# Score and broadcast products on 128 rows instead of 64 or 4, with the local-attention scores as hi/lo sums

## The chip, the cores and the metric

The kernel runs on one core of one Trainium2 chip. It computes two layers of one model and one layer of a second for 256 tokens in a single launch. The metric is the device time of one execution in microseconds, as the median of several runs.

## The reference, cut to what matters

The inputs are 256 tokens of 1024 channels, float32 throughout. Each layer is a chain of large products (feed-forward blocks of 2816 hidden channels, projections in and out) around a token mixer. Three mixers matter here.

Layer A is an mLSTM: its scores are weighted by `exp` of a running maximum of gate sums, for 4 heads, and that maximum (a row of 256 tokens for each head) has to reach all 128 rows of keys.

Layer B is a sliding-window attention with 16 query heads of 64 channels, in two groups of 8 that share one key head each. A block of 128 queries sees its own block of keys and the one before it:

```python
s = jnp.einsum('bqhgd,bkhd->bhgqk', qn, kn)
s = jnp.where(valid, s, -jnp.inf)
m = jnp.maximum(jnp.max(s, axis=-1, keepdims=True), sink)
p = jnp.exp(s - m)
denom = jnp.sum(p, axis=-1, keepdims=True) + jnp.exp(sink - m)
return jnp.einsum('bhgqk,bkhd->bqhgd', p / denom, vn)
```

The second model's layer is a state-space mixer (SSD) with 32 heads of 64 channels, whose scores are weighted by a decay between two tokens:

```python
acum = jnp.cumsum(dtc * a, axis=1)
seg = acum[:, :, None] - acum[:, None, :]
decay = jnp.exp(jnp.where(causal, seg, -jnp.inf))
...
scores = cb[..., None] * decay
```

## The kernel before

Weights come from memory in chunks of 128 x 1024 elements through SyncE's queue (`load`, L314), five chunks ahead. `prepare` splits each chunk into `hi`, a rounded copy in the type fp32r, by ScalarE (L324), and `lo`, the rest, by VectorE (recorded at the helper's line L122). Activations are split in the same way. A large product is then three fp32r matmuls into one PSUM bank: hi by hi, hi by lo, lo by hi. `gemm` does so with tokens as the stationary side and 512 moving columns (L418 to L420), `gemm_ch` with channels as the stationary side and 256 moving columns (L440 to L442). A product of plain float32 operands, without the split, appears in the trace as two matmul passes; an fp32r product and a transpose (L453, L625, against `ident`) appear as one.

Everything else is called side work. `later` queues generators, `defer` delays a function by a number of ticks, and `gemm` and `gemm_ch` call `tick` between their chunks, which runs what is due and takes steps of the generators at a set `pace`. `pipeline` starts one unit at each step and moves a started unit on every second step. The framework then orders each engine's instructions with this program order as their priority, so that a transpose can land in the middle of another unit's score products. Each engine executes its own list in order.

Three kinds of side product use fewer than 128 rows of TensorE's array, that is, operands that lie on fewer than 128 partitions:

- L1010 in `swa_units`, the scores of layer B. A unit takes heads of one parity, because two heads share a 128-row transposed block: even heads lie on rows 0 to 63 and odd heads on rows 64 to 127. `kv_evac` puts the keys on both halves (`kd`, L966), transposes them and copies them into `bkt` (L971), `bq_evac` transposes the queries and copies them (L983). Both are plain float32. The first block of queries (t = 0) sees 128 keys and has two units of four heads for each group, the second (t = 1) sees 256 and has four units of two heads. With two groups that makes four units of the first kind and eight of the second.
- L806 in `score_head`: the row of running maxima of head `hh`, one of the first 4 rows of `m_t`, is spread over 128 rows by a one-hot stationary operand.
- L1227 in `ssd_unit`: the cumulated decays `act_t` (hi parts on 32 rows, lo parts on the next 32) are spread in the same way by a column of `pick`, twice in each of 16 units. `step_chain` makes `act_t` by a product with the identity (L1124) and a copy.

After the scores, a unit of layer B takes the masked maximum (L1013, VectorE), the exponential (L1019, ScalarE), four transposes (L625) and the products with the values (L1032). All of this draws on one pool of 31 slots of 128 x 512 elements (`slot`); powers for the norms run on GpSimd (L504, L508).

Of the kernel before, what the change touches and what calls it, by code (L numbers as in the profile page):

```python
# [17 lines left out]
P = 128  # L18
# [44 lines left out]
class Operand:  # L63
    """A transposed activation, rows of K on the partitions, as an exact sum hi + lo."""
# [11 lines left out]
class Chunk:  # L76
    """One weight transfer of 1024 elements a partition and the products its columns take part in."""
# [8 lines left out]
def hybrid_kernel(ctx: ExitStack, tc: tile.TileContext, *aps, names=None):  # L86
# [54 lines left out]
    # ------------------------------------------------------------ constants  # L141
# [23 lines left out]
    # parameters by channel, transposed once  # L165
# [33 lines left out]
    # rows on every partition  # L199
# [3 lines left out]
    # ------------------------------------------------------------ weights  # L203
# [131 lines left out]
    # Work that the products hide: steps of generators and delayed calls, taken between the chunks.  # L335
# [38 lines left out]
    def pipeline(units, dist):  # L374
        """Starts a unit at each step; a unit goes on to its next stage every dist steps."""
# [15 lines left out]
    def gemm(chunks, xop, evac, groups=None, by_key=False):  # L391
        """Token-major products: evac(tok, key, psum) after each accumulation."""
# [36 lines left out]
    def gemm_ch(chunks, xop, evac):  # L429
        """Channel-major products of 512 columns: evac(pair, psum) with two tiles of 128 channels."""  # L430
# [17 lines left out]
    # ------------------------------------------------------------ activations  # L448
    def split_t(src, nk, dsts):
        """src [tokens, nk*128] transposed, as hi and lo in dsts (APs of [P, nk, 128])."""  # L450
        ps = bank()
        for i in range(nk):
            pe.transpose(out=ps[:, i * P:(i + 1) * P], in_=src[:, i * P:(i + 1) * P], identity=ident)  # L453
        v = ps[:, 0:nk * P].rearrange("p (a b) -> p a b", a=nk)
        act.copy(out=dsts[0], in_=v)
        tt(dsts[1], v, dsts[0].bitcast(F32), ALU.subtract)
# [9 lines left out]
    def direct_block(op, tok, k0, ps, nk):  # L466
        """An operand from a psum that already holds it transposed."""
# [7 lines left out]
    class NormT:  # L475
        """The normed residual, transposed, for products of either kind."""
# [23 lines left out]
    def inv_rms(sums):  # L500
        """(sums[0] + sums[1] + EPS) ** -0.5 of two columns"""
# [8 lines left out]
    def normed(src, gains, put):  # L510
        """src(j) are the two halves of a row; put(j, normed half)"""
# [20 lines left out]
    def residual_gemm(chunks, xop, scale, after, tail=TAIL):  # L532
        """residual += scale * product; after(tok) when a tile is whole"""
# [15 lines left out]
    def norm_after(row, queue=nc.sync):  # L549
        """An operand to be filled by the gemm before, and the function that fills it."""  # L550
# [25 lines left out]
    def log1p_small(o, e, n):  # L576
        """log(1 + e) for 0 <= e <= 1, as 2 atanh(e / (2 + e))"""
# [18 lines left out]
    # ------------------------------------------------------------ memory attention  # L596
# [3 lines left out]
    def head_norm(pieces, n_heads, d):  # L600
        """rms over each head of d columns, of psum pieces side by side; returns a slot"""
# [58 lines left out]
    def mem_unit(t, hp, queries, po, y, k0):  # L660
        """two heads of the attention over the memory for one tile of tokens"""
# [37 lines left out]
    # ------------------------------------------------------------ first block  # L699
# [29 lines left out]
    # ---- layer A: mLSTM  # L729
# [17 lines left out]
    m_t = slot()  # L747

# [51 lines left out]
    def score_head(hh):  # L800
# [5 lines left out]
        pe.matmul(out=bc[:, 0:SEQ], lhsT=ident[0:4, hh:hh + 1].to_broadcast([4, P]), rhs=m_t[0:4, 0:SEQ],  # L806
# [79 lines left out]
    # ---- rotary tables  # L886
# [44 lines left out]
    # ---- layer B: sliding window attention  # L931
    def rope(x3, t, nh):
        """x3 [P, nh, 64] in place"""
# [22 lines left out]
    bkt, bv = slot(), slot()  # L956
# [3 lines left out]
    def kv_evac(t, key, ps):  # L960
# [8 lines left out]
        def go():  # L969
            tk = transposes(kd, 2)  # L970
            dve.tensor_copy(out=bkt.rearrange("p (g t) -> p g t", g=2)[:, :, t * P:(t + 1) * P],  # L971
                            in_=tk[:, 0:SEQ].rearrange("p (g t) -> p g t", g=2))
# [3 lines left out]
    def bq_evac(g):  # L976
        def evac(t, key, ps):
            qn = qk_norm(ps, t, 8, b_gq)

            def go():  # L980
                tq = transposes(qn, 4)
                q = slot()
                act.copy(out=q, in_=tq)  # L983
                qts[t, g] = q
# [3 lines left out]
    def swa_units(t, g):  # L988
        """eight heads of one key head for one block of queries, a bank of scores at a time"""
# [4 lines left out]
        sets = [[h0 + par + 2 * i for i in range(per)] for h0 in range(0, 8, 2 * per) for par in range(2)]  # L994
# [3 lines left out]
        def unit(n, hs):  # L998
            while (t, g) not in qts or len(kv_ready) <= t:
                yield  # L1000
            qt = qts[t, g]
# [5 lines left out]
            cols = slice(hs[0], hs[-1] + 1, 2)  # L1007
            for i, hh in enumerate(hs):
                half = slice(64 * (hh % 2), 64 * (hh % 2) + 64)
                pe.matmul(out=s[:, i * w:(i + 1) * w], lhsT=qt[half, (hh // 2) * P:(hh // 2 + 1) * P],  # L1010
                          rhs=bkt[half, g * SEQ:g * SEQ + w], start=True, stop=True)
# [47 lines left out]
    # ------------------------------------------------------------ second block  # L1059
# [12 lines left out]
    acs = const.tile([P, 2, 2, 32], F32R, name="acs")  # L1072
    act_t = const.tile([64, SEQ], F32R, name="act_t")
    pick = const.tile([64, 32], F32R, name="pick")
# [18 lines left out]
    def step_chain():  # L1093
# [29 lines left out]
        for c in range(2):  # L1123
            pe.matmul(out=at_[0:64, c * P:(c + 1) * P], lhsT=acs[:, c, :, :].rearrange("p b c -> p (b c)"), rhs=identr,  # L1124
                      start=True, stop=True)
        act.copy(out=act_t, in_=at_[0:64, 0:SEQ])
        tt(pick, ident[0:64, 0:32], ident[0:64, 32:64], ALU.add)
# [5 lines left out]
    def conv_silu(ps, tile_i, dst):  # L1133
        """four taps along the tokens, bias and silu: dst [P, SEQ]"""
# [82 lines left out]
    def ssd_unit(g, hp):  # L1217
        """the decays of two heads over both blocks of tokens, and what they give within a block"""
# [178 lines left out]
```

## Time and profile before

| what | value |
|---|---|
| median of 3 runs | 1620.25 us (1619.86 to 1621.65) |
| span of the profiled execution | 1618.5 us (the page lists its span alone, no other time of it) |
| TensorE matmul busy | 1599.2 us, 99% |
| TensorE weight load busy | 1339.0 us, 83% |
| VectorE busy | 966.7 us, 60% |
| ScalarE busy | 822.5 us, 51% |
| GpSimd busy | 40.7 us, 3% |
| TensorE's part of the chain that ended last | 94% |
| mean granted TensorE clock | 0.997 of full speed |

Matmuls are pipelined, so the duration of one overlaps the next. What one costs in a stream is read from the distance between the starts of neighbours, not from its duration. In the timeline view neighbours of one line are merged into one row, with their count behind the x and the time from the first start to the last end as its length. The forms such as 64\*128 give the rows and columns of the array that the instruction uses.

### The profile page before, as it was taken

How to read it: one execution, taken by the hardware profiler on the slowest of the kernel's cores; microseconds unless marked ns; L12 is line 12 of the kernel's file. 1: busy time of each engine (PE TensorE's matmuls, PEld its weight loads, DVE VectorE, ACT ScalarE, POOL GpSimd, SP SyncE). 2: the span in 40 equal slices, each digit the busy share in tenths (PEclk: the TensorE clock that was granted, in tenths of full speed). 3: DMA queues.
4: the chain of work that ended last, by engine and by line, in shares of the span. 5: the costliest groups of instructions: out<-in, count | busy, mean ns of one | idle time of the engine just before them, and what ended most of it. 6: DMA issues, size and time to landing. Idle time of an engine off the chain costs nothing.

```text
span 1618.5 us, 21426 instructions
## 1 busy us (share of the span) xinstructions
PE 1599.2 (99%) x8124; PEld 1339.0 (83%) x8124; DVE 966.7 (60%) x1372; ACT 822.5 (51%) x1170; POOL 40.7 (3%) x72
## 2 busy tenths in 40 slices
PE   9999999999999999999999999999999999999998
PEld 7888898788888888888788888889899988888886
DVE  6555475558555555546765655368788864575552
ACT  6444365546444444444564544357856553454442
POOL 0000010100000000001100000000000000000000
PEclk9999999999999999999999999999999999999999
DMA  8665374446656566564333766565455566466560
GB/s 271 209 188 196 115 263 144 156 130 211 192 184 196 168 197 187 188 196 164 122 88 108 223 193 195 156 197 184 156 158 145 155 195 182 156 221 188 188 198 27
DMA packets 126971, 282.80 MB, mean 175 GB/s; under 512 B 12286, under 2 KB 23698, under 8 KB 126868
## 3 DMA queue, kind: packets, MB, share of 16 engines
q1 hardware_dynamic: 126868, 281.43, 55.0%
q8 instruction: 64, 1.05, 0.3%
q14 instruction: 39, 0.32, 0.1%
HBM read 280.34 MB, written 1.05 MB: 174 GB/s over the span
## 4 chain that ended last, share of the span: by engine, by line
PE 94%; DVE 2%; issue 1%; ACT 1%; DMA 1%; POOL 1%; SPq 0%; POOLq 0%; ACTq 0%; DVEq 0%
PE ps L418 25%; PE ps L420 25%; PE ps L419 25%; PE ps L440 3%; PE ps L441 3%; PE ps L442 3%; PE ps L453 3%; DMA raw<-in_ffn_w_in_dram 1%; PE ps L625 1%; PE ps L1010 1%; PE ps L1252 1%; POOL t L508 1%; PE ps L1032 1%; DVE wlo L122 1%; ACT whi L324 1%
## 5 line engine op out<-in xcount | busy, mean ns | idle before, releaser
L122 DVE TENSOR_TENSOR wlo<-raw,whi 128x1024 fp32r<-128x1024 f32 (+1 forms) x521 | 628.5, 1213 | 440.3 <-ACT whi L324 433.8
L324 ACT CAST whi<-raw 128x1024 fp32r<-128x1024 f32 (+1 forms) x521 | 543.0, 1044 | 556.4 <-PE ps L420 474.3
L418 PE MATMUL ps<-whi,xh 128*128 128x512 f32 (+2 forms) x1168 | 459.5, 394 | 3.0 <-DVE s L122 1.5
L420 PE MATMUL ps<-whi,xl 128*128 128x512 f32 (+2 forms) x1168 | 451.3, 387 | 0.3 <-DVE xl L122 0.2
L419 PE MATMUL ps<-wlo,xh 128*128 128x512 f32 (+2 forms) x1168 | 450.8, 386 | 0.0
L418 PE MATMUL ps<-whi,s 128*128 128x512 f32 x696 | 278.9, 401 | 0.3 <-ACT s L1329 0.3
L419 PE MATMUL ps<-wlo,s 128*128 128x512 f32 x696 | 274.5, 394 | 0.0
L420 PE MATMUL ps<-whi,s 128*128 128x512 f32 x696 | 274.1, 394 | 0.0
L418 PEld LDWEIGHTS ps<-whi,xh 128*128 128x128 f32 x1168 | 219.7, 188 | 48.1 <-DVE s L122 2.3
L420 PEld LDWEIGHTS ps<-whi,xl 128*128 128x128 f32 x1168 | 219.5, 188 | 45.9 <-DVE xl L122 0.9
L419 PEld LDWEIGHTS ps<-wlo,xh 128*128 128x128 f32 x1168 | 219.9, 188 | 41.5 <-issue 0.3
L420 PEld LDWEIGHTS ps<-whi,s 128*128 128x128 f32 x696 | 130.7, 188 | 30.7
L418 PEld LDWEIGHTS ps<-whi,s 128*128 128x128 f32 x696 | 130.8, 188 | 30.4 <-ACT s L1329 0.8
L419 PEld LDWEIGHTS ps<-wlo,s 128*128 128x128 f32 x696 | 130.9, 188 | 28.7
L440 PE MATMUL ps<-xh,whi 128*128 128x256 f32 x448 | 129.8, 290 | 0.0
L441 PE MATMUL ps<-xl,whi 128*128 128x256 f32 x448 | 127.6, 285 | 0.0
L442 PE MATMUL ps<-xh,wlo 128*128 128x256 f32 x448 | 127.6, 285 | 0.0
L440 PEld LDWEIGHTS ps<-xh,whi 128*128 128x128 f32 x448 | 86.4, 193 | 1.7 <-issue 0.2
L441 PEld LDWEIGHTS ps<-xl,whi 128*128 128x128 f32 x448 | 86.4, 193 | 0.4 <-issue 0.2
L442 PEld LDWEIGHTS ps<-xh,wlo 128*128 128x128 f32 x448 | 86.2, 193 | 0.1
L453 PE MATMUL ps<-ident,s 128*128 128x128 f32 x444 | 66.7, 274 | 2.0 <-DVE s L131 2.0
L453 PEld LDWEIGHTS ps<-ident,s 128*128 128x128 f32 x444 | 54.3, 141 | 16.4 <-issue 1.9
(211 smaller groups left out, 971.8 us busy)
## 6 DMA issues: line engine op xcount, KB each, us to landing
raw<-in_ffn_w_in_dram SPq DMA_DIRECT2D x160, 512.0 KB, 4.7
raw<-in_ffn_w_out_dram SPq DMA_DIRECT2D x88, 512.0 KB, 3.4
raw<-in_w_in_dram SPq DMA_DIRECT2D x80, 512.0 KB, 4.1
raw<-in_a_w_in_dram SPq DMA_DIRECT2D x24, 512.0 KB, 4.6
raw<-in_w_gate_dram SPq DMA_DIRECT2D x44, 256.0 KB, 3.1
raw<-in_w_up_dram SPq DMA_DIRECT2D x44, 256.0 KB
raw<-in_w_down_dram SPq DMA_DIRECT2D x22, 512.0 KB, 3.4
raw<-in_ffn_w_in_dram SPq DMA_DIRECT2D x32, 256.0 KB, 3.3
```

The source lines that it names most:

```text
L122: (eng or dve).tensor_tensor(out=o, in0=a, in1=b, op=op)
L324: act.copy(out=c.hi[:, 0:n], in_=c.raw[:, 0:n])
L418: pe.matmul(out=o, lhsT=xh, rhs=wh, start=first, stop=False)
L419: pe.matmul(out=o, lhsT=xh, rhs=wl, start=False, stop=False)
L420: pe.matmul(out=o, lhsT=xl, rhs=wh, start=False, stop=last)
L440: pe.matmul(out=o, lhsT=wh, rhs=xh, start=kt == 0 and j % 2 == 0, stop=False)
L441: pe.matmul(out=o, lhsT=wh, rhs=xl, start=False, stop=False)
L442: pe.matmul(out=o, lhsT=wl, rhs=xh, start=False, stop=kt == nk - 1 and j % 2 == 1)
L453: pe.transpose(out=ps[:, i * P:(i + 1) * P], in_=src[:, i * P:(i + 1) * P], identity=ident)
L508: pool_e.tensor_tensor(out=o, in0=a, in1=mhalf[:, 0:1].to_broadcast([P, n]), op=ALU.pow)
L625: pe.transpose(out=ps[:, i * P:(i + 1) * P], in_=src[:, i * P:(i + 1) * P], identity=ident)
L1010: pe.matmul(out=s[:, i * w:(i + 1) * w], lhsT=qt[half, (hh // 2) * P:(hh // 2 + 1) * P], rhs=bkt[half, g * SEQ:g * SEQ + w], start=True, s ...
```

## The change

All three products get operands on 128 rows. For L806 the tile `m_t` is cleared on GpSimd and all its rows take part. For L1227 `acs` is widened to 128 columns with zeros in the upper half, so that `act_t` and `pick` have 128 rows.

For L1010 the keys of each group go into a tile of two halves: half u = 0 holds the keys on rows 0 to 63 and zeros elsewhere, half u = 1 holds them on rows 64 to 127. A stationary block of 128 rows (two heads) against both halves gives the scores of both heads side by side. The keys are split into `kh` and `kl` by four ScalarE copies and four VectorE subtractions for each block of tokens, where one copy stood; each of the four query tiles gets a `ql` by one more subtraction. A pair of heads is then three fp32r products of 256 moving columns (t = 0) or 512 (t = 1), and a unit holds neighbouring heads. Four slots are cleared on GpSimd for the keys, where `bkt` had one; the queries hold two slots for each tile instead of one.

Comments and docstrings that the diff also removes are left out here.

```diff
     gg, efloor, fcum = little(), little(), little()
     m_t = slot()
+    pool_e.memset(m_t[:, 0:SEQ], 0.0)
...
-        pe.matmul(out=bc[:, 0:SEQ], lhsT=ident[0:4, hh:hh + 1].to_broadcast([4, P]), rhs=m_t[0:4, 0:SEQ],
+        pe.matmul(out=bc[:, 0:SEQ], lhsT=ident[:, hh:hh + 1].to_broadcast([P, P]), rhs=m_t[:, 0:SEQ],
                   start=True, stop=True)
...
-    bkt, bv = slot(), slot()
+    bv = slot()
+
+    kpad = [[slot(F32R).rearrange("p (u t) -> p u t", u=2) for _ in range(2)] for _ in range(2)]
+    for kp in kpad[0] + kpad[1]:
+        pool_e.memset(kp.bitcast(F32), 0.0)
...
             tk = transposes(kd, 2)
-            dve.tensor_copy(out=bkt.rearrange("p (g t) -> p g t", g=2)[:, :, t * P:(t + 1) * P],
-                            in_=tk[:, 0:SEQ].rearrange("p (g t) -> p g t", g=2))
+            for u in range(2):
+                rows_u = slice(64 * u, 64 * u + 64)
+                for g in range(2):
+                    kh, kl = (kp[rows_u, u, t * P:(t + 1) * P] for kp in kpad[g])
+                    kt = tk[rows_u, g * P:(g + 1) * P]
+                    act.copy(out=kh, in_=kt)
+                    tt(kl, kt, kh.bitcast(F32), ALU.subtract)
...
                 tq = transposes(qn, 4)
-                q = slot()
-                act.copy(out=q, in_=tq)
-                qts[t, g] = q
+                qh, ql = slot(F32R), slot(F32R)
+                act.copy(out=qh, in_=tq)
+                tt(ql, tq, qh.bitcast(F32), ALU.subtract)
+                qts[t, g] = (qh, ql)
...
-        sets = [[h0 + par + 2 * i for i in range(per)] for h0 in range(0, 8, 2 * per) for par in range(2)]
+        sets = [list(range(h0, h0 + per)) for h0 in range(0, 8, per)]
...
-            cols = slice(hs[0], hs[-1] + 1, 2)
-            for i, hh in enumerate(hs):
-                half = slice(64 * (hh % 2), 64 * (hh % 2) + 64)
-                pe.matmul(out=s[:, i * w:(i + 1) * w], lhsT=qt[half, (hh // 2) * P:(hh // 2 + 1) * P],
-                          rhs=bkt[half, g * SEQ:g * SEQ + w], start=True, stop=True)
+            cols = slice(hs[0], hs[-1] + 1)
+            kh, kl = (kp[:, :, 0:w] for kp in kpad[g])
+            for i in range(0, per, 2):
+                pair = slice((hs[i] // 2) * P, (hs[i] // 2 + 1) * P)
+                o2 = s[:, i * w:(i + 2) * w].rearrange("p (a b) -> p a b", a=2)
+                pe.matmul(out=o2, lhsT=qh[:, pair], rhs=kh, start=True, stop=False)
+                pe.matmul(out=o2, lhsT=qh[:, pair], rhs=kl, start=False, stop=False)
+                pe.matmul(out=o2, lhsT=ql[:, pair], rhs=kh, start=False, stop=True)
...
-    acs = const.tile([P, 2, 2, 32], F32R, name="acs")
-    act_t = const.tile([64, SEQ], F32R, name="act_t")
-    pick = const.tile([64, 32], F32R, name="pick")
+    acs = const.tile([P, 2, 4, 32], F32R, name="acs")
+    pool_e.memset(acs.bitcast(F32), 0.0)
+    act_t = const.tile([P, SEQ], F32R, name="act_t")
+    pick = const.tile([P, 32], F32R, name="pick")
...
-            pe.matmul(out=at_[0:64, c * P:(c + 1) * P], lhsT=acs[:, c, :, :].rearrange("p b c -> p (b c)"), rhs=identr,
+            pe.matmul(out=at_[:, c * P:(c + 1) * P], lhsT=acs[:, c, :, :].rearrange("p b c -> p (b c)"), rhs=identr,
                       start=True, stop=True)
-        act.copy(out=act_t, in_=at_[0:64, 0:SEQ])
-        tt(pick, ident[0:64, 0:32], ident[0:64, 32:64], ALU.add)
+        act.copy(out=act_t, in_=at_[:, 0:SEQ])
+        tt(pick, ident[:, 0:32], ident[:, 32:64], ALU.add)
...
-            pe.matmul(out=sb[:, i * SEQ:(i + 1) * SEQ], lhsT=pick[:, hd:hd + 1].to_broadcast([64, P]), rhs=act_t,
+            pe.matmul(out=sb[:, i * SEQ:(i + 1) * SEQ], lhsT=pick[:, hd:hd + 1].to_broadcast([P, P]), rhs=act_t,
                       start=True, stop=True)
```

## Rows read from the trace of the kernel before

**Rows 1.** The page's chain that ended last, by engine.

```profile
PE 94%; DVE 2%; issue 1%; ACT 1%; DMA 1%; POOL 1%; SPq 0%; POOLq 0%; ACTq 0%; DVEq 0%
```

**Rows 2.** Windows: layer B's attention, then SSD; length, PE, PEld, DVE, ACT, POOL, clock.

```profile
780.00:835.00 55.00, 54.36 (x306) 42.01 (x305) 36.06 (x143) 34.43 (x95) 5.28 (x4) 1.00 0.26 79
...
1095.00:1290.00 195.00, 194.96 (x1456) 182.78 (x1457) 164.54 (x297) 132.75 (x217) 5.50 (x6) 1.00 0.52 156
```

**Rows 3.** Timeline (start, length) of TensorE around a unit of L1010, t = 0.

```profile
808.46 0.61 PE L625 MATMUL ps<-ident,s 128*128 128x128 f32 x4
809.00 1.16 PE L1010 MATMUL ps<-s,s 64*128 64x128 f32 x8
810.08 0.50 PE L418 MATMUL ps<-whi,xh 128*128 128x512 f32 x1
810.42 0.39 PE L419 MATMUL ps<-wlo,xh 128*128 128x512 f32 x1
810.65 0.40 PE L420 MATMUL ps<-whi,xl 128*128 128x512 f32 x1
```

**Rows 4.** The same for a unit of t = 1, in one piece.

```profile
825.37 0.60 PE L625 MATMUL ps<-ident,s 128*128 128x128 f32 x4
825.90 1.13 PE L1010 MATMUL ps<-s,s 64*128 64x256 f32 x4
826.96 0.66 PE L625 MATMUL ps<-ident,s 128*128 128x128 f32 x4
```

**Rows 5.** The same for a unit of t = 1 split by transposes.

```profile
788.28 0.27 PE L625 MATMUL ps<-ident,s 128*128 128x128 f32 x1
788.48 0.70 PE L1010 MATMUL ps<-s,s 64*128 64x256 f32 x2
789.10 0.44 PE L625 MATMUL ps<-ident,s 128*128 128x128 f32 x2
789.47 0.70 PE L1010 MATMUL ps<-s,s 64*128 64x256 f32 x2
```

**Rows 6.** Timeline of TensorE around one visit to L1227.

```profile
1254.22 0.28 PE L441 MATMUL ps<-xl,whi 128*128 128x256 f32 x1
1254.34 0.28 PE L442 MATMUL ps<-xh,wlo 128*128 128x256 f32 x1
1254.55 0.50 PE L1227 MATMUL ps<-act_t,pick 64*128 64x256 f32 x2
1254.98 0.39 PE L440 MATMUL ps<-xh,whi 128*128 128x256 f32 x1
1255.20 0.28 PE L441 MATMUL ps<-xl,whi 128*128 128x256 f32 x1
```

**Rows 7.** Timeline of TensorE: the last visit to L806, and L668.

```profile
255.77 1.12 PE L806 MATMUL ps<-s,ident 4*128 4x256 f32 x4
256.82 0.50 PE L418 MATMUL ps<-whi,xh 128*128 128x512 f32 x1
...
834.50 1.03 PE L668 MATMUL ps<-mem_kt,s 128*128 128x256 f32 x4
835.36 0.60 PE L453 MATMUL ps<-ident,s 128*128 128x128 f32 x4
```

**Rows 8.** Timeline before layer B's first scores: ScalarE, VectorE, TensorE.

```profile
779.06 0.27 ACT L967 COPY s<-ps 128x128 f32<-128x128 f32 x1
780.84 1.04 ACT L324 CAST whi<-raw 128x1024 fp32r<-128x1024 f32 x1 [1.52 <-PE ps L420]
...
781.43 0.42 DVE L971 COPY s<-ps 128x256 f32<-128x256 f32 x1
...
781.91 1.16 PE L1010 MATMUL ps<-s,s 64*128 64x128 f32 x8 [0.64 <-DVE s L971]
```

**Rows 9.** GpSimd: a clear by line, and its first head norm of layer B.

```profile
L152 POOL MEMSET mask_a<- 128x256 f32 x1 | 0.3, 311 | 0.0
...
757.95 1.65 POOL L508 TENSOR_TENSOR t<-t,mhalf 128x8 f32<-128x8 f32 x1 [3.42 <-DVE t L128]
```

More of the change, by code (lines that the diff above doesn't have):

```diff
@@ L1000, in unit @@
                 yield
-            qt = qts[t, g]
+            qh, ql = qts[t, g]
             if not hold:
```

## The prediction

> **What bounds the kernel now.** I read the chain that ended last first: TensorE holds 94% of it [rows 1]. So time saved on TensorE is saved at the end, if in that stretch nothing else is just behind it. The windows say how near the others are. In layer B's attention TensorE is busy for 54.36 of 55 us, VectorE for 36.06 and ScalarE for 34.43; in the SSD stretch for 194.96 of 195, with VectorE at 164.54 [rows 2]. The reader is to see that TensorE has no holes there, and that VectorE is close in the second stretch, not in the first. The granted clock is 1.00 in both, which is the 2.4 GHz level, so nothing is to be gained or lost there unless holes appear.
>
> Then the timeline of TensorE around the three products, where distances between starts count. Three base distances first. An fp32r product of 512 columns takes 0.23 us (810.42 to 810.65 [rows 3]), one of 256 columns 0.12 (1254.22 to 1254.34 [rows 6]), and a float32 pass of 256 columns on full rows 0.86 / 4 = 0.215 (834.50 to 835.36 [rows 7]). A transpose is put at 0.11, an estimate from the four of [rows 3], which take 0.54 with the disturbed start of what follows.
>
> What is to be seen is that an instruction on 64 rows disturbs its neighbours. At L1227 the start comes 0.21 after L442 where 0.12 is normal, the two products take 0.43 instead of 0.24, and the first L440 after them takes 0.22 instead of 0.12 [rows 6]. After L1010 the first L418 takes 0.34 instead of 0.23 [rows 3]. So each change of the row count costs about 0.1 us before the first product and 0.1 after it, and a visit of any length pays for two changes, about 0.4 us. L1227 is fp32r before and after, and its columns stay the same: there the change of rows is the only thing that the edit touches.
>
> **The change part by part.**
>
> *L1010, four units of t = 0.* The four transposes from 808.46 would be through at 808.90; the unit starts at 809.00: 0.10. It takes 1.08 to the start of L418, and L418 loses 0.11 [rows 3]. Together 1.29. After: two pairs by three fp32r products of 256 columns, 6 x 0.12 = 0.72. Four units gain 4 x 0.57 = 2.3 us.
>
> *L1010, eight units of t = 1.* Four stand in one piece, by the timeline: the start is 0.09 late (825.37 + 0.44 against 825.90), and the unit takes 1.06 [rows 4], together 1.15. Four are split by transposes into two visits: 0.09 late, 0.62, then two transposes that take 0.37 where 0.22 is normal (0.15), and 0.62 again [rows 5], together 1.48. After, each is three products of 512 columns, 0.69. Gain 4 x 0.46 + 4 x 0.79 = 5.0 us. A switch hidden behind a transpose is left out of this, so it is a lower value.
>
> *L1227, 16 units of two products.* One visit costs 0.09 + 0.43 + 0.10 = 0.62 [rows 6]; after, 2 x 0.12 = 0.24. Two of the units stand together and share a visit, so 15 x 0.38 = 5.7 us.
>
> *L806.* The last visit takes 1.05 for four passes [rows 7]; with 0.10 and 0.11 at its ends, as at L1010, 1.26, against 4 x 0.215 = 0.86 on full rows. Three visits of this cost, 3 x 0.40 = 1.2 us.
>
> *L1124.* Its two products load 128 columns instead of 64. Between nothing and twice 0.12 is lost; the nearest row is that of a load of 128 columns in a stream of 256, where the whole product takes 0.12, and half of it was there before: 0.1 us.
>
> *Key tiles.* This adds to a wait that is on the path: TensorE stood for 0.64 us until the copy at L971 was done [rows 8]. In its place stand four ScalarE copies and four VectorE subtractions, each reading the one before. The nearest row of a copy is L967, 0.27 for 128 columns; a subtraction I put below L971's 0.42 for twice the columns, at 0.22. If the copies come ahead of the weight cast at 780.84, in ScalarE's hole of 1.52, they are done by 780.4 (779.33 + 4 x 0.27), and the first of the new products needs no more than that. The second needs `kl`, the third subtraction after 781.43: 782.1 instead of 781.9. By then one product is done, so this end is about nothing. If they stand behind the cast, they begin at 781.88, the third ends at 782.7 and its subtraction at 783.0: 1.1 late, less the 0.12 done: 1.0. I take 0.4, nearer to the first because L971 stands ahead of that cast's own subtraction on VectorE. What is late next is the masked maximum L1013, which nothing on TensorE needs for microseconds, as other units' transposes come between.
>
> *Query splits.* Four subtractions of 512 columns on VectorE, about 0.7 each by its rate in L971 (0.42 for 256), 2.7 us in a stretch where it is idle for 19 of 55 us [rows 2]. Nothing, with that cover; up to 2.7 without it.
>
> *Clears on GpSimd.* The clear of 256 columns took 0.31 [rows 9], so four of 512 take at most 4 x 0.62 = 2.5 us. They stand ahead of the first head norm at 757.95, before which GpSimd was idle for 3.42 us [rows 9]. Nothing, if the slots are free in time; up to 2.5 if not, because the query transposes wait for that norm. The clears of `m_t` and `acs` fall into GpSimd's idle time (5.5 busy of 195 in the SSD stretch [rows 2]): nothing.
>
> Sum: 2.3 + 5.0 + 5.7 + 1.2 - 0.1 - 0.4 = 13.7 us. The profiled span is 1618.5, so the new one should be 1604.8. The median of the runs lies 1.75 above that span, and I keep this distance: 1606.5 us, 0.85% faster.
>
> **A rule that speaks against it.** In [rows 3] eight passes on 64 rows take 1.08 us, 0.135 each, and a full-row pass of the same columns is put at 0.11: two heads on 64 rows are not done side by side. The Trainium skill ("TensorEngine Tiling (Array Packing)", Theoretical Speedup) holds that a contraction of 64 or less, laid on two row tiles, can run up to twice as fast, so zeros on half the rows would throw half the array away. The row doesn't bear this out for this kernel, since the heads of a unit lie on the same half.
>
> **The rivals.**
>
> *Row halves overlap after all, 1 in 100.* If the passes of a unit ran two at a time elsewhere, the removed ones would be worth half: 32 passes of 0.11 and 32 of 0.215, 10.4 us, so 5.2 of the gain would fall away, and 1611.7 us would remain. Against it: in [rows 4] four passes take 1.06, more than on full rows. This is the rule named in the part above.
>
> *Layer B takes half back, 10 in 100.* The clears come late (2.5), the keys stand behind the cast (0.6 more), and VectorE's splits of the queries have no cover (2.7): 5.8 in all, 1612.3 us. For it: GpSimd's order puts the clears ahead of the norm, and the slots for them come out of a pool that the feed-forward block before has just used. Against it: VectorE's 19 idle microseconds.
>
> *VectorE becomes the bound in the SSD stretch, 6 in 100.* It is busy for 164.54 of 195; with 5.7 us less of TensorE it is at 87%, and bursts could hold TensorE. Then the 5.7 of L1227 are lost: 1612.2. Against it: TensorE stands for 0.04 us in all of that stretch.
>
> *The rows are not what costs, 3 in 100.* If the late starts came from something else in these instructions (the broadcast operand, the change from fp32r to float32), only the passes themselves would change: 4 x (8 x 0.11 - 0.72) + 8 x (4 x 0.215 - 0.69) = 2.0 us, less 0.5: 1618.8, no change that can be told. Against it: L1010 has no broadcast, L1227 is fp32r, and both show the same 0.1 us.
>
> *The slots run out, slower, 5 in 100.* The change holds seven more of the 31: four for the keys against one, and four `ql`. A unit whose tile `o` or `pt` gets no slot can't start until an earlier unit's values are done. If a unit held TensorE for 2 us, the 12 units and the four of the memory attention after them would lose 32 us: 1638. It decides from 13.7 + 3.2 over 16 units, 1.1 us each. Against it: before the change TensorE stands for 0.64 us in that stretch, so there is no sign that the pool was near its end.
>
> *More than forecast, 3 in 100.* The split units come together, or the wait for the keys goes: at most the 0.64 and 0.4, and some 1.5 of switches left out: 1603.5.
>
> **How the numbers follow.** The forecast has 72 in 100, with a range of its own of 1604.5 to 1609 (the key chain's two ends, one late clear). The whole range takes in the rivals near 1612 and the better case: 1603 to 1612.4, leaving out the slots, the rows and some of the forecast's tails. A measurement of this kernel can tell about 0.2%, 3.2 us, from no change. Faster: 72 + 1 + 10 + 6 + 3 = 92; same: 3; slower: 5.
>
> **What the profile after would show.** Right: no form with 64 or 4 rows on the three lines; an L440 after L1227 at 0.12, an L418 after the scores at 0.23; score units of 0.72 and 0.69 from start to start; 24 products of 256 and 24 of 512 columns in place of the 64 passes; TensorE's idle time ahead of the first scores at 0.6 to 1.7 us. Wrong: new waits of TensorE on `s` in 780 to 835, a first head norm later than 4 us after the norm before it, waits in the SSD stretch, or neighbours that still lose 0.1 us with all rows in use.

## The result and the profile after

The kernel now takes 1611.49 us, median of four runs (1610.2 to 1613.29), against 1620.08 before (1619.86 to 1621.65): a ratio of 0.9947, with an interval of 0.9935 to 0.996, so 8.6 us or 0.53% faster. Forecast were 1606.5 with a range of 1603 to 1612.4. The profiled execution took 1610.49 us with a span of 1608.5, where 1618.5 stood before: the span lost 10.0 of the 13.7 us forecast.

To see where they went, I took stretches between starts of the same weight products in both traces, and set the idle time of TensorE beside them:

| stretch | before | after | gained | forecast |
|---|---|---|---|---|
| layer A's gates (241st to 361st start of L418) | 117.5 | 115.0 | 2.5 | 1.2 |
| layer B's attention (961st to 1081st start of L418) | 130.1 | 127.3 | 2.8 | 2.3 + 5.0 - 0.4 = 6.9 |
| SSD (65th start of L440 to 1441st of L418) | 223.1 | 218.3 | 4.8 | 5.7 - 0.1 = 5.6 |

In the profile after, L806 has become L807, L1010 is L1023 (high by high), L1024 (high by low) and L1025 (low by high), L1227 is L1242, the maximum and the exponential of the softmax are L1027 and L1033, and the products with the values are L1046. None of these lines has a form with fewer than 128 rows any more; eight small products elsewhere still do (L715 on 1 row, L777 on 4, L1111 on 32). The page's chain that ended last:

```profile
PE 92%; DVE 3%; issue 2%; ACT 2%; DMA 1%; POOL 1%; SPq 0%; POOLq 0%; DVEq 0%; ACTq 0%
```

Against [rows 1] TensorE lost two points, and VectorE, ScalarE and "issue" took one each. The windows tell in which stage (length, PE, PEld, DVE, ACT, POOL, clock). After:

```profile
740.00:850.00 110.00, 103.72 (x598) 86.90 (x597) 83.16 (x242) 68.60 (x162) 15.47 (x13) 1.00 0.40 130
780.00:835.00 55.00, 51.86 (x314) 43.38 (x315) 40.37 (x150) 38.49 (x108) 6.12 (x4) 1.00 0.28 87
1095.00:1290.00 195.00, 194.96 (x1460) 184.01 (x1459) 166.45 (x297) 133.55 (x218) 5.97 (x7) 1.00 0.54 162
```

Before, for the first of them:

```profile
740.00:850.00 110.00, 106.52 (x594) 86.32 (x593) 80.07 (x233) 66.33 (x152) 12.89 (x10) 1.00 0.40 129
```

TensorE's idle time in these 110 us rose from 3.48 to 6.28; an idle time that is given for a run below is that of this window. The SSD stretch has TensorE busy for 194.96 of 195 as in [rows 2]. Layer B's 55 us, which had 0.64 us without it, now have 3.14. The timeline of TensorE (start, length, and in brackets the idle time with what ended it) shows two of these holes, a unit of t = 0 and one of t = 1 (the first product of each and what follows its last), and a visit in the SSD stretch:

```profile
791.99 0.39 PE L418 MATMUL ps<-whi,xh 128*128 128x512 f32 x1
793.59 0.33 PE L625 MATMUL ps<-ident,s 128*128 128x128 f32 x1 [1.21 <-ACT s L1033]
...
808.71 0.50 PE L418 MATMUL ps<-whi,s 128*128 128x512 f32 x1 [1.12 <-ACT s L455]
...
810.32 0.38 PE L1023 MATMUL ps<-s,s 128*128 128x256 f32 x1 [0.20 <-DVE s L122]
...
811.13 0.40 PE L420 MATMUL ps<-whi,s 128*128 128x512 f32 x1
...
814.07 0.39 PE L1023 MATMUL ps<-s,s 128*128 128x512 f32 x1
...
814.76 1.00 PE L1046 MATMUL ps<-s,s 128*128 128x64 f32 x8
...
1245.66 0.28 PE L442 MATMUL ps<-xh,wlo 128*128 128x256 f32 x1
1245.78 0.40 PE L1242 MATMUL ps<-act_t,pick 128*128 128x256 f32 x2
1246.01 0.28 PE L440 MATMUL ps<-xh,whi 128*128 128x256 f32 x1
1246.13 0.28 PE L441 MATMUL ps<-xl,whi 128*128 128x256 f32 x1
```

L1242 starts 0.12 after L442, takes 0.23 for two, and the first L440 after it takes 0.12: the late starts of [rows 6] are gone. A unit of t = 0 takes 0.81 (810.32 to 811.13) and one of t = 1 takes 0.69 (814.07 to 814.76) where [rows 3, 4] had 1.08 and 1.06. The first lines are what was not there before: holes of 1.21 and 1.12 us. Among the waits of TensorE from 740 to 850 (total, times, longest) are, after:

```profile
PE ps L625 <- DVE s L122: 2.8, 3, 1.5
PE ps L625 <- ACT s L1033: 1.4, 2, 1.2
PE ps L418 <- ACT s L455: 1.1, 1, 1.1
PE ps L1023 <- issue: 0.5, 1, 0.5
```

and before, all that exceed 0.2 us:

```profile
PE ps L625 <- DVE t L128: 1.6, 1, 1.6
PE ps L625 <- DVE s L122: 1.0, 1, 1.0
PE ps L1010 <- DVE s L971: 0.6, 1, 0.6
```

Two waits of 1.0 and 1.5 us on L122 lie at 760 and 772 us, ahead of the changed products, and have their like before; a wait ahead of the first scores is there in both. New are the exponential of the softmax (L1033) and ScalarE's copy of a transposed attention result (L455), which the output projection of layer B reads. What is ahead of that exponential, on the timelines of VectorE and ScalarE:

```profile
791.64 0.15 DVE L122 TENSOR_TENSOR t<-t,rows 128x4 f32<-128x4 f32 x1
791.71 1.22 DVE L122 TENSOR_TENSOR wlo<-raw,whi 128x1024 fp32r<-128x1024 f32 x1
792.85 0.16 DVE L126 TENSOR_SCALAR t<-t 128x4 f32<-128x4 f32 x1
793.04 0.40 ACT L1033 ACTIVATE s<-s,t 128x128 f32<-128x128 f32 x1 [1.80 <-DVE t L126]
```

The softmax's maximum is ready; its sign change (L126) of 128x4 stands behind a weight split of 1.22 us on VectorE, ScalarE waits for the sign change, and TensorE for the exponential.

### The profile page after: what moved, and what is told of

Same layout as the page of the kernel before. It is cut to its first block, busy times and chain, and to the rows that moved or that the text cites. A ratio compares the mean times of both kernels' runs of the same rounds, so it can differ in the third digit from the quotient of the medians.

```text
span 1608.5 us, 21428 instructions
## 1 busy us (share of the span) xinstructions
PE 1585.2 (99%) x8108; PEld 1334.0 (83%) x8108; DVE 969.5 (60%) x1382; ACT 824.4 (51%) x1178; POOL 44.3 (3%) x78
## 4 chain that ended last, share of the span: by engine, by line
PE 92%; DVE 3%; issue 2%; ACT 2%; DMA 1%; POOL 1%; SPq 0%; POOLq 0%; DVEq 0%; ACTq 0%
PE ps L418 25%; PE ps L420 25%; PE ps L419 25%; PE ps L440 3%; PE ps L441 3%; PE ps L442 3%; PE ps L453 3%; DVE wlo L122 1%; POOL t L508 1%; PE ps L1267 1%; DMA raw<-in_ffn_w_in_dram 1%; ACT whi L324 1%; PE ps L625 1%; DVE s L122 1%; PE ps L689 0%
## 5 line engine op out<-in xcount | busy, mean ns | idle before, releaser
L122 DVE TENSOR_TENSOR wlo<-raw,whi 128x1024 fp32r<-128x1024 f32 (+1 forms) x521 | 628.5, 1214 | 439.4 <-ACT whi L324 434.0
L418 PE MATMUL ps<-whi,xh 128*128 128x512 f32 (+2 forms) x1168 | 458.3, 393 | 2.7 <-DVE s L122 1.5
L420 PE MATMUL ps<-whi,xl 128*128 128x512 f32 (+2 forms) x1168 | 450.8, 386 | 1.7 <-DVE xl L122 1.7
L419 PE MATMUL ps<-wlo,xh 128*128 128x512 f32 (+2 forms) x1168 | 450.8, 386 | 0.0
L418 PE MATMUL ps<-whi,s 128*128 128x512 f32 x696 | 278.1, 400 | 1.5 <-ACT s L455 1.1
L419 PE MATMUL ps<-wlo,s 128*128 128x512 f32 x696 | 274.9, 395 | 0.0
L420 PE MATMUL ps<-whi,s 128*128 128x512 f32 x696 | 274.6, 395 | 0.0
L418 PEld LDWEIGHTS ps<-whi,xh 128*128 128x128 f32 x1168 | 219.5, 188 | 46.6 <-DVE s L122 2.2
L420 PEld LDWEIGHTS ps<-whi,xl 128*128 128x128 f32 x1168 | 219.2, 188 | 46.5 <-DVE xl L122 2.1
L419 PEld LDWEIGHTS ps<-wlo,xh 128*128 128x128 f32 x1168 | 219.7, 188 | 41.4
L418 PEld LDWEIGHTS ps<-whi,s 128*128 128x128 f32 x696 | 130.8, 188 | 31.4 <-ACT s L455 1.3
L420 PEld LDWEIGHTS ps<-whi,s 128*128 128x128 f32 x696 | 130.7, 188 | 30.6
L419 PEld LDWEIGHTS ps<-wlo,s 128*128 128x128 f32 x696 | 130.9, 188 | 28.8
L440 PE MATMUL ps<-xh,whi 128*128 128x256 f32 x448 | 128.0, 286 | 0.0
L442 PE MATMUL ps<-xh,wlo 128*128 128x256 f32 x448 | 126.7, 284 | 0.0
L440 PEld LDWEIGHTS ps<-xh,whi 128*128 128x128 f32 x448 | 85.7, 191 | 0.3 <-issue 0.2
L442 PEld LDWEIGHTS ps<-xh,wlo 128*128 128x128 f32 x448 | 85.6, 191 | 0.0
L122 DVE TENSOR_TENSOR s<-ps,s 128x512 fp32r<-128x512 f32 (+2 forms) x100 | 61.6, 628 | 13.2 <-ACT s L455 6.0
```

The lines of the kernel that those rows point to most:

```text
L122: (eng or dve).tensor_tensor(out=o, in0=a, in1=b, op=op)
L418: pe.matmul(out=o, lhsT=xh, rhs=wh, start=first, stop=False)
L419: pe.matmul(out=o, lhsT=xh, rhs=wl, start=False, stop=False)
L420: pe.matmul(out=o, lhsT=xl, rhs=wh, start=False, stop=last)
L440: pe.matmul(out=o, lhsT=wh, rhs=xh, start=kt == 0 and j % 2 == 0, stop=False)
L442: pe.matmul(out=o, lhsT=wl, rhs=xh, start=False, stop=kt == nk - 1 and j % 2 == 1)
```

## The experiments

The first theories were **M**, that a change of the rows in use is what costs, and **R**, that only the passes count. For the loss in layer B there were **S**, that the work of the splits on VectorE and ScalarE makes the chain late, and **C**, that a faster TensorE runs into the softmax chain, which was just in time before. Ratios are to the kernel before on the same chip.

**The SSD part alone.** Gate and layer B stay as before; of the change only this:

```diff
-    acs = const.tile([P, 2, 2, 32], F32R, name="acs")
+    acs = const.tile([P, 2, 4, 32], F32R, name="acs")
+    pool_e.memset(acs.bitcast(F32), 0.0)
...
-            ... lhsT=pick[:, hd:hd + 1].to_broadcast([64, P]), rhs=act_t,
+            ... lhsT=pick[:, hd:hd + 1].to_broadcast([P, P]), rhs=act_t,
```

> The kernel before with the 128-row edit of the SSD broadcast alone (L1124, L1227). Theory M (each change of the row count costs TensorE about 0.1 us before and 0.1 us after): all 15 visits lose both changes, 4.7 to 5.7 us faster than before, and the stretch from 1095 us to the end of the SSD units is shorter by 4.5 to 5 us as in the changed kernel. Rival R (the rows are not what costs): within 0.5 us of before.

1613.95 us (1613.86 to 1617.15) against 1620.81: 0.996 (0.9948 to 0.9973), 6.5 us faster (4.4 to 8.4). The SSD stretch is 218.3, 4.8 less; layer B's is 130.2, as before. R falls: same passes, same columns, only the rows differ. That the time gained more than the stretch is not the edit's: layer A's stretch is 115.8 in this profile, where 117.5 stood before, with nothing changed in it (the clock, see below).

**Layer B's part alone.** Gate and SSD go back.

```diff
-        ... lhsT=ident[:, hh:hh + 1].to_broadcast([P, P]), rhs=m_t[:, 0:SEQ],
+        ... lhsT=ident[0:4, hh:hh + 1].to_broadcast([4, P]), rhs=m_t[0:4, 0:SEQ],
...
-    act_t = const.tile([P, SEQ], F32R, name="act_t")
+    act_t = const.tile([64, SEQ], F32R, name="act_t")
```

> The changed kernel with the gate broadcast and the SSD broadcast undone, so layer B's scores alone are changed. If the parts add up, 2.5 to 3.5 us faster than before, about 1617, with TensorE standing for some 3 us between 780 and 835 us instead of 0.64. If the parts help or hinder each other (order of the instructions, clock), it differs from this by over 1.5 us.

1615.94 us (1614.94 to 1619.94): 0.9971 (0.996 to 0.9982), 4.7 us faster, more than the 2.5 to 3.5 expected; with the 6.5 of the SSD part that is more than the change's 8.6, but within the intervals. Layer A's stretch is again shorter without an edit, 116.2. Layer B's stretch is 126.9, 3.2 less than before, SSD's 223.1 as before, and TensorE stands for 5.78 of the 110 us (before: 3.48, after: 6.28). So the loss belongs to layer B's own part.

**The splits' work laid on the kernel before.** Its products stay. The key copies go through ScalarE as after the change, and the subtractions are made, but nobody reads what they give.

```diff
-            dve.tensor_copy(out=bkt.rearrange("p (g t) -> p g t", g=2)[:, :, t * P:(t + 1) * P],
-                            in_=tk[:, 0:SEQ].rearrange("p (g t) -> p g t", g=2))
+            for u in range(2):
+                for g in range(2):
+                    ...
+                    act.copy(out=bkt[rows_u, at], in_=kt)
+                    tt(kl_[rows_u, at], kt, bkt[rows_u, at], ALU.subtract)
...
+                tt(slot(F32R), tq, q, ALU.subtract)
```

> The kernel before, its 64-row products kept, with the split work of the change laid on ScalarE and VectorE: eight copies of 64 rows for the keys on ScalarE, eight subtractions of 64 rows and four of 512 columns on VectorE, whose results nobody reads. Theory S (the split work delays the chain maximum, exponential, transpose, and TensorE waits): 2 to 3.5 us slower than before, with holes of TensorE of 2.5 us or more in layer B. Theory C (the chain of the softmax on VectorE and ScalarE was just behind TensorE already, and TensorE, now faster, runs into it): within 0.7 us of before.

1622.47 us against 1620.81: 1.001 (1.0001 to 1.0019), 1.7 us slower (0.2 to 3.1), an interval that reaches into both theories. Layer B's stretch grows by 2.1 to 132.2 (the run of the SSD part alone, with layer B as before, had 130.2), the idle time from 3.48 to 4.58. Among the new waits between 780 and 835 us are these (L1026 is the exponential here, L1017 the scores):

```profile
PE ps L625 <- ACT s L1026: 0.7, 2, 0.4
PE ps L418 <- ACT s L455: 0.5, 1, 0.5
...
PE ps L1017 <- DVE s L122: 0.3, 1, 0.3
```

So this work alone opens holes ahead of the same two lines, L625 and L418, with TensorE as slow as before. C does not explain them; they are smaller than S has them.

**High parts alone.** This leaves out the products with `kl` and `ql` and their subtractions, so the scores have the precision of one fp32r product.

```diff
-                pe.matmul(out=o2, lhsT=qh[:, pair], rhs=kh, start=True, stop=False)
-                pe.matmul(out=o2, lhsT=qh[:, pair], rhs=kl, start=False, stop=False)
-                pe.matmul(out=o2, lhsT=ql[:, pair], rhs=kh, start=False, stop=True)
+                pe.matmul(out=o2, lhsT=qh[:, pair], rhs=kh, start=True, stop=True)
```

> The changed kernel with the hi by hi products alone in layer B's scores: the lo parts of keys and queries are neither made nor multiplied, so the scores are less exact. TensorE loses 5.5 us of passes (24 of 0.12 and 24 of 0.23 become 8 and 8) and VectorE the eight short and four long subtractions. Theory S: the holes go with the subtractions, and the time falls by 7 to 8 us against the changed kernel, to about 1604. Theory C: the chain still sets the pace in the first half of layer B, holes of TensorE grow by most of what its passes lose, and the time falls by 3 us or less, to 1608.5 or more.

1608.77 us (1605.83 to 1609.7): 0.9921 (0.9908 to 0.9935), by the two ratios 4.2 us below the change (2.7 by the medians, which were not taken side by side), for 8 x 2 x 0.12 + 8 x 2 x 0.23 = 5.6 us of products left out. TensorE's idle time in the 110 us grew by 1.1 to 7.38, their granted clock is 0.98, so half clock took its part too, and among the waits are:

```profile
PE ps L1021 <- DVE s L122: 1.6, 1, 1.6
PE ps L625 <- ACT s L1029: 1.4, 2, 1.2
...
PE ps L418 <- ACT s L455: 1.0, 1, 1.0
```

L1029 is the exponential here and L1021 the scores. The holes of 1.2 and 1.0 us are still there though no lo part is made, which S excludes; but they did not grow by most of the 5.6 us, as C had it, and the new one stands elsewhere. What the run shows is that with TensorE faster still the two holes don't need the subtractions.

**Padded keys in float32**, no splits at all, and one float32 product for a pair.

```diff
+                    act.copy(out=kpad[g][rows_u, u, t * P:(t + 1) * P], in_=tk[rows_u, g * P:(g + 1) * P])
...
+                pe.matmul(out=o2, lhsT=qt[:, pair], rhs=kpad[g][:, :, 0:w], start=True, stop=True)
```

> The changed kernel with layer B's scores on 128 rows but in plain float32: padded keys and queries are not split, a pair of heads is one product of two passes. TensorE's passes cost 12 x 0.86 = 10.3 us instead of 8.4, so 2 us more; VectorE loses all subtractions (4.9 us) and the copy into the key tile, ScalarE keeps its eight short copies. Theory S (split work makes the holes): holes of TensorE between 780 and 835 us fall from 3.1 to under 1 us, and the time is 0.5 to 1.5 us below the changed kernel. Theory C (TensorE runs into the softmax chain): holes shrink only by what the passes grow, to 1 to 2 us, and the time is within 0.7 us of the changed kernel.

1610.5 us (1609.84 to 1611.72): 0.9939 (0.9925 to 0.9952), not to be told from the change; the time alone decides nothing. Layer B's stretch is 126.2, the idle time 4.61. Between 780 and 835 us TensorE stands for 1.79 us, and the only wait there is

```profile
PE ps L625 <- ACT s L1026: 1.7, 2, 1.1
```

where L1026 is the exponential. That is what C expected (1 to 2 us) and not S (under 1); the wait for L455 is gone.

**Steps of a unit further apart** in the order: a unit's next step comes after three other starts of units, not two.

```diff
-DIST_B = 2
+DIST_B = 3
```

> The changed kernel with units of layer B moved on at every third step instead of every second (DIST_B = 3), so that a unit's transposes are put behind more weight products. Theory C: the holes ahead of the transposes (1.2 us at 793.6) close, 1 to 2.5 us faster than the changed kernel. Theory S: the late work is late for everybody, within 0.7 us. Later units could delay the output projection of layer B: then the hole at 808.7 grows, and the gain is lost.

1616.19 us (1615.28 to 1617.1): 0.9973 (0.9963 to 0.9982), by the two ratios 4.2 us slower than the change, where C expected a gain. Layer B's stretch is 131.7. The hole at 793.6 did close, but a longer one came in another place, and what followed ran slowly, as its timeline of TensorE shows:

```profile
810.57 3.64 PE L1046 MATMUL ps<-s,s 128*128 128x64 f32 x16 [2.22 <-DVE t L1027]
```

and the window behind it:

```profile
812.00:818.00 6.00, 6.00 (x33) 5.71 (x33) 3.90 (x21) 2.66 (x12) 0.76 (x1) 0.59 0.00 0
```

A granted clock of 0.59 over 6 us is mostly the 1.2 GHz level: the hole of 2.22 us was paid for twice.

**96 rows** for the SSD broadcast.

```diff
-    act_t = const.tile([P, SEQ], F32R, name="act_t")
+    act_t = const.tile([96, SEQ], F32R, name="act_t")
...
-            ... lhsT=pick[:, hd:hd + 1].to_broadcast([P, P]), rhs=act_t,
+            ... lhsT=pick[:, hd:hd + 1].to_broadcast([96, P]), rhs=act_t,
```

> The changed kernel with the SSD broadcast on 96 rows (three blocks of 32 instead of four). If any use of fewer than 128 rows costs a change, the distances around the visits are as before: 0.21 ahead of it, 0.34 or 0.22 for the first product after it, 4.8 us lost in that stretch. If what counts is that the array is divided into row tiles of 64 or 32, 96 rows are handled as 128: 0.12 ahead and after, no loss.

One run of 1609.64 us; the SSD stretch is 218.3, as with 128 rows. Its timeline of TensorE:

```profile
1244.86 0.28 PE L442 MATMUL ps<-xh,wlo 128*128 128x256 f32 x1
1244.98 0.40 PE L1242 MATMUL ps<-act_t,pick 96*128 96x256 f32 x2
1245.22 0.28 PE L440 MATMUL ps<-xh,whi 128*128 128x256 f32 x1
1245.34 0.28 PE L441 MATMUL ps<-xl,whi 128*128 128x256 f32 x1
```

Distances of 0.12, 0.24 and 0.12: no late start on either side. So it is not fewer than 128 rows that costs; 96 are free, 64 and 4 are not.

**Another pace of the work between units.** `PACE_B` is the number of attention steps for each tick of the weight products.

```diff
-PACE_B = 0.7
+PACE_B = 1.0
```

> The changed kernel with PACE_B = 1.0 instead of 0.7: a step of layer B's units at each tick, so scores, exponentials and transposes all come earlier in program order, and closer together. Theory C: the units' transposes meet their exponentials sooner, holes ahead of them grow (by 1 us or more), while the hole ahead of the output projection at 808.7 (1.1 us) goes; together within 1.5 us of the changed kernel, holes moved. Theory S: holes unchanged in place and size.

1609.56 us (1607.06 to 1612.59): 0.9933 (0.9921 to 0.9946). Layer B's stretch is 125.7, 1.6 less than after the change, and the wait for L455 is gone; those for L1033 stay (1.7 us in three, 1.4 in two before this edit). C had them grow by 1 us or more, S had no change; neither came out whole.

**The same pace with padded float32 keys**, as in the two edits above.

> The changed kernel with layer B's scores in plain float32 on 128 rows (as in the run with padded float32) and PACE_B = 1.0 (as in the run with that pace). If the two gains come from different holes (no split work on VectorE, and no wait ahead of the output projection), they add up: layer B's stretch gains about 5 us against before instead of 2.7, and the time is 1608 to 1609.5. If both only remove the hole at 808.7, nothing is added to either alone: 1609.5 to 1610.5.

1608.87 us (1607.43 to 1611.81): 0.9928 (0.9915 to 0.9942). Idle time 3.43, as before the change, and layer B's stretch 125.8, 4.2 less than before and no less than with the pace alone (125.7): the time lies where it was expected if the gains add up, the stretch doesn't bear that out. This has the lowest median of the versions that compute the whole reference, 11.7 us below the kernel before; from the change (0.9935 to 0.996) the intervals don't part it.

**A pace between** (`PACE_B = 0.85`):

> The changed kernel with PACE_B = 0.85. Theory C: the holes depend on where the program order puts the units' transposes and the output projection's first operand among the weight products, so a pace between gives holes in other places and a time between 1608 and 1613, not on a line between those of 0.7 and 1.0. Theory S: the time is that of the changed kernel within 0.7 us.

1612.04 us (1608.92 to 1613.34): 0.9946 (0.9933 to 0.9958). Inconclusive, as the time fits both theories; idle time 5.61, and layer B's stretch, 126.4, lies between those of the two paces.

**The sign change on ScalarE**, so that it doesn't stand behind a weight split:

```diff
-            ts(nmx[:, cols], mx[:, cols], -1.0, ALU.mult)
+            act.activation(out=nmx[:, cols], in_=mx[:, cols], func=AF.Copy, scale=-1.0)
```

> The changed kernel with the sign change of the masked maximum (12 small instructions, 0.17 us each) on ScalarE instead of VectorE. In the changed kernel that instruction stood behind a weight subtraction of 1.22 us on VectorE at 791.71, while ScalarE was idle for 1.80 us. Theory C: the hole ahead of the transposes at 793.6 shrinks by about 1 us, other waits on exponentials go too, and layer B's stretch falls by 1 to 2 us. Theory S: the hole stays, since the subtractions of the splits are still there. The time falls by 0 to 2 us, to 1609.5 to 1611.5.

1611.37 us (1609.88 to 1612.42): 0.9945 (0.9931 to 0.9959), no gain. Its timeline of TensorE has these holes:

```profile
792.98 0.33 PE L625 MATMUL ps<-ident,s 128*128 128x128 f32 x1 [0.96 <-ACT s L1033]
...
799.55 0.44 PE L625 MATMUL ps<-ident,s 128*128 128x128 f32 x2 [0.82 <-ACT s L1033]
...
808.33 0.50 PE L418 MATMUL ps<-whi,s 128*128 128x512 f32 x1 [0.38 <-ACT s L455]
...
810.61 0.39 PE L1023 MATMUL ps<-s,s 128*128 128x256 f32 x1 [0.88 <-DVE s L122]
```

The hole of 1.21 became one of 0.96, the one of 1.12 became 0.38, and 0.82 and 0.88 opened elsewhere: idle time 6.25 against 6.28. Layer B's stretch is 127.2, 0.1 less than after the change, where C had 1 to 2 us. So one late instruction was not the cause by itself; that all of the chain is about as long as TensorE's work is argued from this, not measured.

**Both**, the sign change on ScalarE and the pace of 1.0:

> The same with PACE_B = 1.0. That pace alone took away the hole ahead of the output projection and left two waits on exponentials (1.7 us of idle time). If the sign change on ScalarE takes those, layer B's stretch falls from 125.7 to 124 to 125 us and the time to 1607 to 1609; if it only moves them, 1609.5 as with the pace alone.

1610.58 us (1607.85 to 1612.23): 0.9935 (0.992 to 0.9949), no better than the pace alone: layer B's stretch is 126.7, where 124 to 125 was expected if the waits went.

## Why the prediction was right in its mechanism and its gain about 5 us too large

*A change of rows costs at both sides: right.* The SSD part alone shows it, since only its rows differ, and the run with 96 rows bounds it. The Trainium skill ("TensorEngine Tiling (Array Packing)", Key Properties) says that TensorE drains when the tiling mode changes, and its section Available Configurations lists row tiles of 128, 64 and 32 rows. The trace agrees as far as it goes: the visit on 64 rows of [rows 6] lost 0.38 us, about half of it at each end, and the one on 96 rows loses nothing.

*L1227: a term mis-sized, 5.7 less 0.1 forecast, 4.8 measured.* The visit that I costed is one of the dear ones. From the start of what runs ahead of a visit to the second product behind it, the 15 visits gained 5.0 us together: five 0.38 to 0.40 each, seven 0.32 to 0.34, three 0.20 to 0.27. The seven follow L1252 (L1267 after the change). Around one of them, the run ahead and the second product behind, before:

```profile
1151.31 1.00 PE L1252 MATMUL ps<-s,s 128*128 128x64 f32 x8
...
1153.00 0.40 PE L419 MATMUL ps<-wlo,xh 128*128 128x512 f32 x1
```

and after:

```profile
1145.45 1.00 PE L1267 MATMUL ps<-s,s 128*128 128x64 f32 x8
...
1146.81 0.39 PE L419 MATMUL ps<-wlo,xh 128*128 128x512 f32 x1
```

The 1.69 us from the first of these starts to the second, with the visit and one L418 between them, became 1.36. The 0.2 us between 5.0 and 4.8 I did not take apart.

*L806: 1.2 forecast, and its rows bear it out.* The last visit now:

```profile
253.43 0.39 PE L420 MATMUL ps<-whi,xl 128*128 128x512 f32 x1
253.65 1.02 PE L807 MATMUL ps<-s,ident 128*128 128x256 f32 x4
254.33 0.58 PE L418 MATMUL ps<-whi,xh 128*128 128x512 f32 x1
254.75 0.39 PE L419 MATMUL ps<-wlo,xh 128*128 128x512 f32 x1
```

From L420 to L419 are 1.32 us, and without the two weight products (0.23 each) 0.86, as forecast. The stretch gained 2.5, but in the profile before the clock falls in it: after a hole of 1.98 us the window shows 0.70, which it doesn't after the change (below). By the distances in it that is worth about 1.5, so about 1.0 is left for L806. The runs of the SSD part alone and of layer B's part alone, which leave L806 as it was and keep the clock at 1.00 there, say the same: 115.8 and 116.2 us against 115.0. It also means that of the 10.0 us of the span, about 8.5 are the change's, close to the 8.6 of the medians.

*L1010's products: right.* Units of 0.81 and 0.69 where 0.72 and 0.69 were forecast: 4 x 0.48 + 4 x 0.46 + 4 x 0.79 = 6.9 us for 7.3.

*The failed step: "Nothing, with that cover" for the query splits, and "What is late next is the masked maximum L1013, which nothing on TensorE needs for microseconds".* The stretch gained 2.8 where its products gained 6.9. So 4.1 us were given back, against the 0.4 that I had; 2.8 of them stand in the windows as idle time (6.28 less 3.48), and a part of the rest beside the holes: from 791.99 to 793.59 are 1.60 us, of which 0.23 are the L418's and only 1.21 are counted as idle. The prediction had named the sign itself, "new waits of TensorE on `s` in 780 to 835": those on L1033, L455 and L122 are there. I had read "VectorE is idle for 19 of 55 us" as cover. But a share of busy time says nothing of latency: the path from the scores through maximum, sign change and exponential to the next transposes, and on to the copy that the output projection reads, runs through two in-order queues with weight work of 1.0 to 1.2 us in between. Before the change it ended before TensorE came for it; by how much, no row shows. The wait ahead of the first scores, for which I had 0.4 more, is shorter: 0.52 against 0.64 [rows 8].

*S or C stays open in its shares.* The waits between 780 and 835 us, without the one ahead of the first scores, come to nothing before the change and to 3.0 us after it. The splits' work alone, where TensorE was slow, made 1.5 of them and cost 2.1 us of the stretch (1622.47). Without any split, a faster TensorE made 1.7 (padded float32, 1610.5). So both contribute, in these two runs by about as much; but this second TensorE is some 2 us slower than that of the change, and no run has the change's products without the splits' work, so the shares stay rough. Order alone gave 1.6 us of the stretch back in one profile, and other edits of order or engine moved the holes without removing them.

*The range.* The 1611.49 us lie above the forecast's own 1604.5 to 1609, and inside the whole range only because that was stretched to 1612.4 for rivals which did not come as described. That the whole range held is more luck than foresight. The better case near its lower end is a slip: 1606.5 less 0.64, 0.4 and 1.5 is 1604.0, not 1603.5.

*Rivals.* "Layer B takes half back" came nearest, in its amount and in one of its three terms, the splits without cover (2.7 there; 2.1 of the stretch when laid on the kernel before). The keys were not late, and its late clears didn't happen: GpSimd's four take 1.92 us, and the head norm starts 3.95 us after the norm before it, where it was 3.97 (753.98 to 757.95):

```profile
751.25 0.55 POOL L504 TENSOR_TENSOR t<-t,mhalf 128x1 f32<-128x1 f32 x1 [13.20 <-DVE t L128]
751.75 1.92 POOL L961 MEMSET s<- 128x512 f32 x4
755.20 1.65 POOL L508 TENSOR_TENSOR t<-t,mhalf 128x8 f32<-128x8 f32 x1 [1.52 <-DVE t L128]
```

VectorE did not become the bound in the SSD stretch (0.04 us idle on TensorE, as before), the rows were what costs, and of slots that ran out no wait shows anything. "Row halves overlap" falls with the units' gain, which is that of whole passes; whether heads of both parities, set to run side by side on the two halves of the rows, would overlap, no run tried.

## What to carry to other kernels

In a stream of full-row products, count a visit on 64 rows or fewer with what it and its neighbours lose, here 0.3 to 0.4 us in most places. Rows of zeros that fill it up to 128 cost none of that, and 96 rows cost none either. When the bound engine gets faster in a stage, follow one unit through the other engines from its input to the point where the bound engine needs it: behind idle shares of about 35% lay a chain that became the wait, and together with the splits' new work it took back 4 of 7 us. Holes that depend on order move when one instruction is moved; measure the stretch, not the hole.

## What was not expected of the hardware

A product on 96 rows costs its neighbours nothing, one on 64 does (0.12 against 0.21 between starts).

An fp32r product directly after a float32 one seems dear and is not. In the last visit to L807 the L418 behind it shows 0.42 us to the next start instead of 0.23, but the four float32 passes ahead of it show only 0.68. Together that is 1.10, as 4 x 0.215 + 0.23 = 1.09 gives without any loss.

Holes of about the same length on TensorE are followed by half clock or not. Before, TensorE's timeline, and under it the window behind the hole:

```profile
225.63 0.44 PE L625 MATMUL ps<-ident,s 128*128 128x128 f32 x2 [1.98 <-DVE s L122]
```

```profile
228.00:232.00 4.00, 4.00 (x26) 4.00 (x26) 3.07 (x12) 1.81 (x3) 0.00 (x0) 0.70 1.01 367
```

and after, with the longer hole, the same two views:

```profile
225.91 0.44 PE L625 MATMUL ps<-ident,s 128*128 128x128 f32 x2 [2.15 <-DVE s L122]
```

```profile
228.00:232.00 4.00, 4.00 (x36) 4.00 (x35) 3.24 (x12) 2.54 (x4) 0.00 (x0) 1.00 1.02 382
```

26 products against 36 in the same 4 us. The run with 96 rows has a hole of 1.98 us there too, as long as the one before the change, and keeps 1.00. Such falls are a likely part of the scatter between runs of one kernel: the change's four runs, 1610.2, 1610.49, 1612.48 and 1613.29 us, have mean granted clocks of 0.999, 0.998, 0.997 and 0.995. Where the clock fell is known of the profiled run alone.
